# Wider input stages, value products beside five of them, and gathered rank products in a two-layer mixer on one Trainium2 core

## The chip, the core and the metric

The kernel runs on one core of a Trainium2 chip, in one launch. The time is device microseconds of that core, the median of several executions. PE or TensorE multiplies matrices, DVE (VectorE) and ACT (ScalarE) work on rows of 128 partitions, POOL is GpSimd, and SP's queue issues most of the DMA loads. A raw weight of fp32 is split into a high part and a remainder, both of the type fp32r, and one exact product costs three TensorE products: high times high, high times remainder, remainder times high.

## What is computed

The reference holds two layers. Only the start of the first one is touched here. With `x` and `ctx` of 256 tokens by 2048 channels each:

```python
sh, sc, gt = modulation(c_lat, w_ada[0], b_ada[0], 3)      # silu(c) @ w_ada + b_ada, 2048 channels each
sh_c, sc_c = modulation(c_c, w_ada[0], b_ada[0], 2)
u  = x   * (1.0 + sc)   + sh
uc = ctx * (1.0 + sc_c) + sh_c
k, v, rf, rb, q, gate_b, a_b, a_c, a_x, gate_a = split_cols(u @ w_in_e[0], E_SIZES)
k_c, v_c, rf_c, rb_c = split_cols(uc @ w_in_e[0][:, :2080], E_SIZES[:4])
```

`k` and `v` have 1024 columns, the gate ranks `rf` and `rb` 16 columns each. The keys, values and ranks are needed for `x` and for `ctx`; gated linear attention, a short convolution, an output projection with layer normalisation and the whole second layer follow.

## The kernel before, in words

The contraction over 2048 channels is done in 16 tiles of 128 (`KT`). The modulation of a channel tile has to be known before that tile's input can be multiplied with anything, so the first layer begins in stages, listed in `STAGES` (L58): 1, 1 and then seven times 2 channel tiles.

A stage has two halves. `stage_u` (L362) loads the columns of `x` and `ctx` that belong to its tiles (`load_xc`, L208), loads their shift and scale columns of `w_ada` and multiplies them with silu(c) (`mod_rows`, L264): units of 1 MB go through four raw buffers (`wraw`, L95), and the 16 contraction tiles are summed in four groups of output rows, the product of tile kt in group kt % 4. With n tiles in a stage a unit is 128 x n columns wide and holds 16 / n contraction tiles; a row of it in memory is 512 x n bytes. `to_cols` (L283) copies the four partial rows (ACT, L286) and turns them into columns (L289). Then each tile of the input is transposed (L386, L387), scaled and shifted (L389, L390) and split (L394 to L397). Whenever four tiles are done, the ranks of these four are multiplied (L398 to L409): four products of 32 columns, in the four row groups of one PSUM tile `pr`, and `r_acc` takes their sum.

`stage_k` (L411) multiplies the keys of a stage: two units of 512 columns, for each of them four token tiles (two of `x`, two of `ctx`) with 3 x n products, added into `knat` by DVE (L422). `v_fill` (L439) does the same with the first 512 columns of the values, for two contraction tiles at a time; `FILLS` (L41) puts it behind the stages that end at tiles 2, 4, 6 and 8, so 8 of the 16 contraction tiles are done there. Its split weights lie in buffers of their own (`wide`, L324); all others share four buffers for high parts and four for remainders, each of two contraction tiles by 512 columns (`whp`, `wlp`, L96, L97).

The loop at L563 sets the order: `w_ahead` loads and splits the two key units of the stage before, `stage_u` of this stage, `stage_k` of the stage before, then its fills. A load of values therefore stands behind the modulation weights of the next stage. SP issues the loads of weights in this order, and each waits for one of the four raw buffers. The order of the instructions on every engine is fixed ahead of the run by a scheduler that works with priorities (`prio`, L103) and planned times.

After the stages come the rest of the values (L768: for each half of the columns the units that no fill has done, here 2 and 4, 48 products each), the queries, the attention in the background, the convolution and the projection. Beside every unit of weights `tick` (L605) steps background work: `gate_gen` (L698) and later the attention by a budget, and the modulation of the second layer (`ada_accum`, L522, DVE) by `ada_credit`, 3 steps a unit in the values, fewer later; what is left is done at L1132, ahead of the first normalisation.

Of the kernel before, what the change touches and what calls it, by code (L numbers as in the profile page):

```python
# [9 lines left out]
F32 = mybir.dt.float32  # L10
# [3 lines left out]
ALU = mybir.AluOpType  # L14
# [3 lines left out]
P = 128  # L18
# [14 lines left out]
ADA_0 = {}  # L33
# [7 lines left out]
FILLS = {2: [(0, 0, 2)], 4: [(0, 2, 2)], 6: [(0, 4, 2)], 8: [(0, 6, 2)]}  # L41
FILL_PRIO = 0
# [15 lines left out]
STAGES = (1, 1, 2, 2, 2, 2, 2, 2, 2)  # L58
# [3 lines left out]
def kernel(  # L62
# [96 lines left out]
    # units in the order of their use; loads and splits run ahead of the products  # L159
# [71 lines left out]
    # columns 2, 3: silu of c and c_ctx; a window of 32 columns puts them on the rows 0, 1 or 2, 3 of a product  # L231
# [5 lines left out]
    # columns of colT: see the rows above  # L237
# [26 lines left out]
    def mod_rows(k0, n):  # L264
        """scale (rows 0, 1 of each group of 32) and shift (rows 2, 3) of n channel tiles, summed over every fourth contraction tile"""
# [70 lines left out]
    filled = [[kt + j for f in FILLS.values() for nb, kt, nk in f if nb == n for j in range(nk)] for n in range(2)]  # L336
    V_Q = [[q for q in range(4) if 4 * q not in filled[n]] for n in range(2)]
    for nb in range(2):
        block(W_E, 1024 + nb * 512, V_Q[nb])
# [22 lines left out]
    def stage_u(k0, n):  # L362
        w, n0 = n * P, k0 * P
        xc = xcs.pop(k0, None)
        if xc is None:
            xc = load_xc(k0, n)
        xs, cs = xc[:, 0:2, :], xc[:, 2:4, :]
# [11 lines left out]
        for j in range(n):  # L379
# [5 lines left out]
            for t in range(2):  # L385
                nc.tensor.transpose(out=px[:, t * P : (t + 1) * P], in_=xs[:, t, j * P : (j + 1) * P], identity=ident)  # L386
                nc.tensor.transpose(out=px[:, 256 + t * P : 256 + (t + 1) * P], in_=cs[:, t, j * P : (j + 1) * P], identity=ident)  # L387
# [10 lines left out]
            if i == 3:  # L398
                pr = mp([P, 512], "pr")
                for g in range(4):  # L400
                    kk = kt - 3 + g
                    nc.tensor.matmul(  # L402
                        out=pr[32 * g : 32 * g + 32, :], lhsT=wr[:, kk, :], rhs=quad_u[kk // 2][:, kk % 2, :],
                        start=True, stop=True,
                    )
                if q == 0:
                    nc.vector.tensor_copy(r_acc, pr)
                else:
                    nc.vector.tensor_tensor(out=r_acc, in0=pr, in1=r_acc, op=ALU.add)  # L409
# [13 lines left out]

    wps = []
# [11 lines left out]

    vnat = []

    def v_fill(nb, kt, nk):  # L439
        """a part of the values' contraction, for the gaps that the loads leave"""  # L440
        parts = w_next((W_E, kt, nk, 1024 + nb * 512), 0, 0)
        if not vnat:
            vnat.extend(slot([P, 1024], F32, "vnat") for _ in range(4))
        with prio(FILL_PRIO):
            for m in range(4):
                acc = acc_bank("vfill")
                for j in range(nk):
                    mm3(acc, utile(m, kt + j), parts[j], j == 0, j == nk - 1)
                dst = vnat[m][:, nb * 512 : (nb + 1) * 512]
                if kt == filled[nb][0]:  # L450
                    nc.scalar.copy(dst, acc)
                else:
                    nc.vector.tensor_tensor(out=dst, in0=acc, in1=dst, op=ALU.add)
# [21 lines left out]
    def ada_unit(layer, k0, n0):  # L475
        """four contraction tiles of the modulation's weights, two slots of two"""
# [26 lines left out]
    def ada_rows_gen(layer, dst, engs):  # L503
        """the gate of a layer, on every partition: products on DVE, the sum over the channels with ones"""
# [27 lines left out]
    def ada_cols_gen(layer, n0, dst, bias, one, engs, on_pe=()):  # L532
        """a section as channel columns: products on DVE, or on PE for the column blocks in on_pe"""
# [29 lines left out]
    for n in STAGES:  # L563
        if prev:
            w_ahead(2, SPLIT_0)
        stage_u(k0, n)
        if prev:
            stage_k(*prev)
            pump_ada(ADA_0.get(sum(prev), 0))
            for f in FILLS.get(sum(prev), ()):  # L570
                v_fill(*f)
        elif SPLIT_0:
            with tc.issue_after(arow_ins[0].ins):
                w_ahead(2, 2)
        prev = (k0, n)
        k0 += n
# [45 lines left out]
    def gemm_by_tile(groups, getu, done, budget=0.0, between=None, halves=False):  # L622
        """one token tile behind the other: the first one's sums are done while the second is at work"""
# [711 lines left out]
```

## Time and profile before

| | |
|---|---|
| three runs | 1018.31, 1018.49, 1013.9 us |
| median | 1018.31 us |
| span of the profiled execution | 1014.8 us |
| its own time beside the span | not listed apart; the span lies 3.5 us below the median and 0.9 us above the fastest run |
| TensorE busy | 973.4 us |
| DVE busy | 801.4 us |
| ACT busy | 463.3 us |
| read from memory | 252.41 MB |

All times in the rows below are microseconds from the start of the span. TensorE's records overlap, since one product starts while the one before it is still draining; its cost in a row of products is the distance of their starts. An fp32 product is recorded as two instructions, an fp32r product as one.

### The profile page before, as it was taken

How to read it: one execution, taken by the hardware profiler on the slowest of the kernel's cores; microseconds unless marked ns; L12 is line 12 of the kernel's file. 1: busy time of each engine (PE TensorE's matmuls, PEld its weight loads, DVE VectorE, ACT ScalarE, POOL GpSimd, SP SyncE). 2: the span in 40 equal slices, each digit the busy share in tenths (PEclk: the TensorE clock that was granted, in tenths of full speed). 3: DMA queues.
4: the chain of work that ended last, by engine and by line, in shares of the span. 5: the costliest groups of instructions: out<-in, count | busy, mean ns of one | idle time of the engine just before them, and what ended most of it. 6: DMA issues, size and time to landing. Idle time of an engine off the chain costs nothing.

```text
span 1014.8 us, 14425 instructions
## 1 busy us (share of the span) xinstructions
PE 973.4 (96%) x5718; PEld 768.6 (76%) x5718; DVE 801.4 (79%) x1161; ACT 463.3 (46%) x629; POOL 24.0 (2%) x55
## 2 busy tenths in 40 slices
PE   5899999999999999989999999999999999999995
PEld 4566666778878877877878788887888887778885
DVE  1555556989996999699999879987769968576676
ACT  2422214365684775336563444446554454454340
POOL 2000000000000000000000000000100001000000
PEclk9999999999999999999999999999999999999998
DMA  9987899667786676757767897984887888877532
GB/s 264 327 264 261 284 289 331 203 226 254 249 298 243 199 258 219 258 171 249 245 213 248 290 322 253 323 315 170 292 308 233 277 267 277 284 268 257 175 121 83
DMA packets 150373, 255.45 MB, mean 252 GB/s; under 512 B 5079, under 2 KB 46721, under 8 KB 150305
## 3 DMA queue, kind: packets, MB, share of 16 engines
q1 hardware_dynamic: 146592, 245.13, 72.3%
q0 software_dynamic: 2896, 8.72, 2.7%
q8 instruction: 45, 0.74, 0.3%
q10 hardware_dynamic: 816, 0.68, 0.3%
q14 instruction: 24, 0.19, 0.0%
HBM read 252.41 MB, written 2.10 MB: 251 GB/s over the span
## 4 chain that ended last, share of the span: by engine, by line
PE 43%; DVE 31%; DMA 19%; issue 4%; ACT 3%; SPq 0%; DVEq 0%; ACTq 0%
DMA raw<-in_w_ada_dram 16%; DVE wl L154 11%; DVE aacc L530 8%; PE oacc L191 5%; PE oacc L193 5%; PE oacc L192 5%; PE xacc L193 4%; PE xacc L192 4%; PE xacc L191 4%; PE ada L275 2%; PE kacc L191 2%; PE kacc L193 2%; PE kacc L192 2%; PE pr L402 1%; DMA raw<-in_w_in_e_dram 1%
## 5 line engine op out<-in xcount | busy, mean ns | idle before, releaser
L153 ACT CAST wh<-raw 128x1024 fp32r<-128x1024 f32 (+1 forms) x250 | 257.8, 1044 | 252.6 <-PE xacc L193 97.8
L154 DVE TENSOR_TENSOR wl<-raw,wh 128x1024 fp32r<-128x1024 f32 (+1 forms) x250 | 297.9, 1211 | 40.6 <-ACT wh L153 38.1
L530 DVE SCALAR_TENSOR_TENSOR aacc<-raw,sil,aacc 128x512 f32<-128x512 f32 x240 | 179.5, 748 | 42.6 <-DMA raw<-in_w_ada_dram 38.7
L191 PE MATMUL xacc<-wh,uxh 128*128 128x512 f32 x384 | 152.6, 397 | 0.0
L193 PE MATMUL xacc<-wh,uxl 128*128 128x512 f32 x384 | 151.8, 395 | 0.0
L192 PE MATMUL xacc<-wl,uxh 128*128 128x512 f32 x384 | 150.3, 391 | 0.1
L192 PE MATMUL xacc<-wl,u1h 128*128 128x512 f32 x240 | 94.4, 393 | 3.2 <-DVE wl L154 3.0
L191 PE MATMUL xacc<-wh,u1h 128*128 128x512 f32 x240 | 95.2, 397 | 0.8 <-ACT u1h L1156 0.8
L193 PE MATMUL xacc<-wh,u1l 128*128 128x512 f32 x240 | 93.7, 391 | 0.0
L192 PEld LDWEIGHTS xacc<-wl,uxh 128*128 128x128 f32 x384 | 72.1, 188 | 16.2 <-DVE wl L154 1.0
L193 PEld LDWEIGHTS xacc<-wh,uxl 128*128 128x128 f32 x384 | 72.2, 188 | 15.3 <-issue 0.2
L191 PEld LDWEIGHTS xacc<-wh,uxh 128*128 128x128 f32 x384 | 72.1, 188 | 15.5 <-ACT wh L153 0.5
L422 DVE TENSOR_TENSOR knat<-kacc,knat 128x512 f32<-128x512 f32 x64 | 42.8, 686 | 34.5 <-PE kacc L193 34.3
L192 PEld LDWEIGHTS xacc<-wl,u1h 128*128 128x128 f32 x240 | 45.1, 188 | 16.0 <-DVE wl L154 6.1
L191 PEld LDWEIGHTS xacc<-wh,u1h 128*128 128x128 f32 x240 | 45.1, 188 | 11.2 <-ACT u1h L1156 1.3
L193 PEld LDWEIGHTS xacc<-wh,u1l 128*128 128x128 f32 x240 | 45.1, 188 | 9.5 <-DVE u1l L1157 0.4
L286 ACT COPY arow<-ada 128x256 f32<-128x256 f32 (+1 forms) x9 | 3.1, 349 | 100.8 <-PE ada L275 100.8
L275 PE MATMUL ada<-raw,sil 128*32 128x256 f32 (+1 forms) x576 | 36.4, 382 | 10.8 <-DMA raw<-in_w_ada_dram 10.7
L191 PE MATMUL oacc<-wh,y1h 128*128 128x512 f32 (+1 forms) x120 | 45.5, 379 | 0.0
L193 PE MATMUL oacc<-wh,y1l 128*128 128x512 f32 (+1 forms) x120 | 45.0, 375 | 0.0
L192 PE MATMUL oacc<-wl,y1h 128*128 128x512 f32 (+1 forms) x120 | 45.0, 375 | 0.0
L275 PEld LDWEIGHTS ada<-raw,sil 128*32 128x32 f32 x576 | 17.3, 119 | 27.4 <-issue 12.6
(326 smaller groups left out, 1685.6 us busy)
## 6 DMA issues: line engine op xcount, KB each, us to landing
raw<-in_w_ada_dram SPq DMA_DIRECT2D x96, 1024.0 KB, 6.4
raw<-in_w_in_e_dram SPq DMA_DIRECT2D x54, 1024.0 KB, 5.7
raw<-in_w_in_o_dram SPq DMA_DIRECT2D x32, 1024.0 KB, 6.5
raw<-in_w_out_e_dram SPq DMA_DIRECT2D x16, 1024.0 KB, 7.0
raw<-in_w_out_o_dram SPq DMA_DIRECT2D x16, 1024.0 KB, 5.2
raw<-in_w_in_e_dram SPq DMA_DIRECT2D x18, 512.0 KB, 6.9
raw<-in_w_pool_dram SPq DMA_DIRECT2D x4, 1024.0 KB, 8.1
gt<-in_b_ada_dram POOLq DMA_DIRECT2D x8, 256.0 KB, 4.6
```

Of the source, the lines that this page charges most:

```text
L153: nc.scalar.copy(h, r[:, j : j + w, :])
L154: nc.vector.tensor_tensor(out=l, in0=r[:, j : j + w, :], in1=h.bitcast(F32), op=ALU.subtract)
L191: nc.tensor.matmul(out=acc, lhsT=uh, rhs=wh, start=start, stop=False)
L192: nc.tensor.matmul(out=acc, lhsT=uh, rhs=wl, start=False, stop=False)
L193: nc.tensor.matmul(out=acc, lhsT=ul, rhs=wh, start=False, stop=stop)
L275: nc.tensor.matmul(out=ps[32 * g : 32 * g + 32, :], lhsT=sil[:, kt, 2 - 2 * half : 34 - 2 * half], rhs=r[:, j, :], start=half == 0 and kt ...
L286: arow_ins.append(nc.scalar.copy(a[:, :nw], ps))
L402: nc.tensor.matmul(out=pr[32 * g : 32 * g + 32, :], lhsT=wr[:, kk, :], rhs=quad_u[kk // 2][:, kk % 2, :], start=True, stop=True,)
L422: nc.vector.tensor_tensor(out=dst, in0=acc, in1=dst, op=ALU.add)
L530: e.scalar_tensor_tensor(out=a, in0=r[j], scalar=sc, in1=a, op0=ALU.mult, op1=ALU.add)
```

## The change

The stages become 1, 1, 2, 4, 4, 4. In a four-wide stage a unit of modulation weights is 512 columns wide and holds four contraction tiles. The inputs of such a stage come as two loads of pairs. The values' first 512 columns are multiplied behind the keys of the first five stages, as wide as the stage (12 contraction tiles, of which the first is now behind the first stage), and their split weights use the shared buffers; the later part has 1 and 4 units left. The four rank products of a quarter are issued by `ranks`: the one of the last tile first, the other three behind it, at a raised priority. The values lie in tiles by column halves. All else in the diff is comments and texts taken out.

```diff
-FILLS = {2: [(0, 0, 2)], 4: [(0, 2, 2)], 6: [(0, 4, 2)], 8: [(0, 6, 2)]}
-FILL_PRIO = 0
+PR_PRIO = 200
+V_FILLS = 3
-STAGES = (1, 1, 2, 2, 2, 2, 2, 2, 2)
+STAGES = (1, 1, 2, 4, 4, 4)
...
             specs.append((W_E, k0, n, nb * 512))
+        if k0 + n <= 4 * V_FILLS:
+            specs.append((W_E, k0, n, 1024))
         k0 += n
-        for nb, kt, nk in FILLS.get(k0, ()):
-            specs.append((W_E, kt, nk, 1024 + nb * 512))
-            wide.add(len(specs) - 1)
...
-    for nb in range(2):
-        block(W_E, 1024 + nb * 512, V_Q[nb])
+    block(W_E, 1024, range(V_FILLS, 4))
+    block(W_E, 1536)
...
     def stage_u(k0, n):
-        w, n0 = n * P, k0 * P
-        xc = xcs.pop(k0, None)
-        if xc is None:
-            xc = load_xc(k0, n)
+        w = n * P
+        pairs = [(k, min(2, k0 + n - k)) for k in range(k0, k0 + n, 2)]
+        xts = [xcs.pop(k, None) for k, _ in pairs]
+        xts = [load_xc(*h) if t is None else t for t, h in zip(xts, pairs)]
...
             if i == 3:
-                pr = mp([P, 512], "pr")
-                for g in range(4):
-                    kk = kt - 3 + g
-                    nc.tensor.matmul(
-                        out=pr[32 * g : 32 * g + 32, :], lhsT=wr[:, kk, :], rhs=quad_u[kk // 2][:, kk % 2, :],
-                        start=True, stop=True,
-                    )
...
+                ranks(kt)
+
+    def ranks(kt):
+        pr = mp([P, 512], "pr")
+        def product(g):
+            kk = kt - 3 + g
+            return nc.tensor.matmul(
+                out=pr[32 * g : 32 * g + 32, :], lhsT=wr[:, kk, :], rhs=quad_u[kk // 2][:, kk % 2, :], start=True, stop=True)
+        with prio(-PR_PRIO):
+            first = product(3)
+            with tc.issue_after(first.ins):
+                for g in range(3):
+                    product(g)
...
+    def v_fill(k0, n):
+        parts = w_next((W_E, k0, n, 1024), 0, 0)
+        for m in range(4):
+            acc = acc_bank("vfill")
+            for j in range(n):
+                mm3(acc, utile(m, k0 + j), parts[j], j == 0, j == n - 1)
+            if k0 == 0:
+                nc.scalar.copy(vcols(m, 0), acc)
+            else:
+                nc.vector.tensor_tensor(out=vcols(m, 0), in0=acc, in1=vcols(m, 0), op=ALU.add)
...
             stage_k(*prev)
-            pump_ada(ADA_0.get(sum(prev), 0))
-            for f in FILLS.get(sum(prev), ()):
-                v_fill(*f)
+            if sum(prev) <= 4 * V_FILLS:
+                v_fill(*prev)
...
     for nb in range(2):
         accs = [acc_bank("vacc") for _ in range(4)]
-        gemm(W_E, 1024 + nb * 512, V_Q[nb], range(4), utile, accs, budget=B_V)
+        gemm(W_E, 1024 + nb * 512, range(V_FILLS if nb == 0 else 0, 4), range(4), utile, accs, budget=B_V)
```

## Rows read from the trace of the kernel before

**Rows 1.** The page: busy times, and TensorE and DMA in 40 slices.

```profile
PE 973.4 (96%) x5718; PEld 768.6 (76%) x5718; DVE 801.4 (79%) x1161; ACT 463.3 (46%) x629; POOL 24.0 (2%) x55
...
PE   5899999999999999989999999999999999999995
...
DMA  9987899667786676757767897984887888877532
```

**Rows 2.** Stages: length, busy PE, PEld, DVE, ACT, POOL (instructions), clock, DMA share, GB/s.

```profile
0.00:41.00 41.00, 27.18 (x254) 18.30 (x254) 11.89 (x29) 11.18 (x23) 7.04 (x17) 1.00 1.04 299
41.00:195.00 154.00, 151.61 (x940) 101.01 (x941) 96.62 (x173) 42.91 (x77) 0.41 (x2) 1.00 0.84 274
...
86.00:110.40 24.40, 23.85 (x147) 14.98 (x147) 13.74 (x23) 5.44 (x10) 0.00 (x0) 1.00 0.78 259
...
198.00:270.00 72.00, 71.70 (x326) 58.88 (x323) 65.80 (x96) 42.35 (x65) 0.51 (x5) 1.00 0.75 260
```

**Rows 3.** TensorE's timeline (start, duration): first and last of 24 value products.

```profile
95.98 0.39 PE L191 MATMUL vfill<-swh,uxh 128*128 128x512 f32 x1
...
101.20 0.39 PE L193 MATMUL vfill<-swh,ucl 128*128 128x512 f32 x1
```

**Rows 4.** TensorE's timeline: a unit of modulation weights between two key products.

```profile
80.06 0.39 PE L192 MATMUL kacc<-wl,uxh 128*128 128x512 f32 x1
80.38 1.07 PE L275 MATMUL ada<-raw,sil 128*32 128x256 f32 x16
81.39 0.50 PE L193 MATMUL kacc<-wh,uxl 128*128 128x512 f32 x1
```

**Rows 5.** TensorE's timeline: rank products of the second quarter.

```profile
87.04 1.05 PE L402 MATMUL pr<-u,wr_acc 128*32 128x512 f32 x4
...
88.36 0.40 PE L192 MATMUL kacc<-wl,uxh 128*128 128x512 f32 x1
88.69 1.04 PE L402 MATMUL pr<-u,wr_acc 128*32 128x512 f32 x2
89.67 0.50 PE L193 MATMUL kacc<-wh,uxl 128*128 128x512 f32 x1
90.00 0.40 PE L191 MATMUL kacc<-wh,uxh 128*128 128x512 f32 x1
90.33 1.05 PE L402 MATMUL pr<-u,wr_acc 128*32 128x512 f32 x2
```

**Rows 6.** TensorE's timeline: rank products of the first and the fourth quarter.

```profile
42.65 1.91 PE L402 MATMUL pr<-u,wr_acc 128*32 128x512 f32 x6
...
46.98 1.05 PE L402 MATMUL pr<-u,wr_acc 128*32 128x512 f32 x2
...
171.73 1.92 PE L402 MATMUL pr<-u,wr_acc 128*32 128x512 f32 x6
174.24 1.04 PE L402 MATMUL pr<-u,wr_acc 128*32 128x512 f32 x2
```

**Rows 7.** TensorE's timeline around 41 us; in brackets the idle time before and its releaser.

```profile
39.62 1.07 PE L275 MATMUL ada<-raw,sil 128*32 128x256 f32 x16 [1.88 <-DMA raw<-in_w_ada_dram]
41.18 0.61 PE L289 MATMUL adaT<-sel,arow 128*128 128x4 f32 x4 [0.49 <-ACT arow L286]
...
44.49 0.73 PE L191 MATMUL vfill<-swh,uxh 128*128 128x512 f32 x2
```

**Rows 8.** DMA packets of two stretches: 25 to 40 us, then 730 to 740 us.

```profile
DMA packets 4756, 5.28 MB, mean 352 GB/s; under 512 B 101, under 2 KB 4273, under 8 KB 4755
...
DMA packets 1834, 3.84 MB, mean 384 GB/s; under 512 B 89, under 2 KB 89, under 8 KB 1834
```

**Rows 9.** SP's timeline: loads of two key units and one values unit.

```profile
33.52 4.64 SPq L139 DMA_DIRECT2D raw<-in_w_in_e_dram  x3
```

**Rows 10.** The output projection, columns as in rows 2.

```profile
620.00:640.00 20.00, 20.00 (x90) 16.55 (x89) 18.69 (x25) 7.47 (x9) 0.00 (x0) 1.00 0.77 261
```

**Rows 11.** A wait of TensorE in the attention, and the stretch around it (columns as in rows 2).

```profile
434.46 0.41 PE L965 MATMUL yT<-ident,y 128*128 128x128 f32 x2 [3.63 <-DVE y L959]
...
430.00:440.00 10.00, 6.37 (x22) 4.47 (x21) 8.91 (x26) 2.64 (x4) 0.00 (x0) 0.83 0.34 106
```

More of the change, by code (lines that the diff above doesn't have):

```diff
@@ L384, in stage_u @@
             px = mp([P, 512], "px")
-            for t in range(2):
-                nc.tensor.transpose(out=px[:, t * P : (t + 1) * P], in_=xs[:, t, j * P : (j + 1) * P], identity=ident)
-                nc.tensor.transpose(out=px[:, 256 + t * P : 256 + (t + 1) * P], in_=cs[:, t, j * P : (j + 1) * P], identity=ident)
+            xc, c0 = xts[j // 2], (j % 2) * P
+            for t in range(4):
+                nc.tensor.transpose(out=px[:, t * P : (t + 1) * P], in_=xc[:, t, c0 : c0 + P], identity=ident)
             ux, uc = u[:, kt % 2, 0:256], u[:, kt % 2, 256:512]
@@ L398, in stage_u @@
             if i == 3:
-                pr = mp([P, 512], "pr")
-                for g in range(4):
-                    kk = kt - 3 + g
-                    nc.tensor.matmul(
-                        out=pr[32 * g : 32 * g + 32, :], lhsT=wr[:, kk, :], rhs=quad_u[kk // 2][:, kk % 2, :],
-                        start=True, stop=True,
-                    )
[L406 to L409, printed above, removed]
+                ranks(kt)
[10 more added lines that the diff above has]
+                    product(g)
+        if kt == 3:
+            nc.vector.tensor_copy(r_acc, pr)
+        else:
+            nc.vector.tensor_tensor(out=r_acc, in0=pr, in1=r_acc, op=ALU.add)
     def stage_k(k0, n):
@@ L422, in stage_k, with vcols @@
                     nc.vector.tensor_tensor(out=dst, in0=acc, in1=dst, op=ALU.add)
+    vns = {}
+    def vcols(m, nb, cs=slice(0, 512)):
+        if nb not in vns:
+            vns[nb] = [slot([P, 2, 512], F32, "vnat") for _ in range(2)]
+        return vns[nb][m // 2][:, m % 2, cs]
+    def v_fill(k0, n):
[6 more added lines that the diff above has]
+                nc.scalar.copy(vcols(m, 0), acc)
+            else:
+                nc.vector.tensor_tensor(out=vcols(m, 0), in0=acc, in1=vcols(m, 0), op=ALU.add)
     wps = []
@@ L435, in gate_weights @@
             wps.append(wp)
[L437 to L453, printed above, removed]
     ones = const([P, P], F32, "ones")
@@ L763 @@
         pass
-    if not vnat:
-        vnat.extend(slot([P, 1024], F32, "vnat") for _ in range(4))
     gg = gate_gen()
@@ L948, in gla_gen @@
             for h in range(2):
-                vs = slice((2 * hp + h) * 256, (2 * hp + h + 1) * 256)
-                terms = [(S[:, 2 * h + t, :], vnat[t]), (X[:, 2 * h + 1 - t, :], vnat[1 - t]),
-                         (C[:, 2 * h, isl], vnat[2]), (C[:, 2 * h + 1, isl], vnat[3])]
-                for n, (s_, v_) in enumerate(terms):
-                    nc.tensor.matmul(out=po[:, h, :], lhsT=s_, rhs=v_[:, vs], start=n == 0, stop=n == 3)
+                vs = slice(h * 256, (h + 1) * 256)
+                terms = [(S[:, 2 * h + t, :], t), (X[:, 2 * h + 1 - t, :], 1 - t), (C[:, 2 * h, isl], 2), (C[:, 2 * h + 1, isl], 3)]
+                for n, (s_, m) in enumerate(terms):
+                    nc.tensor.matmul(out=po[:, h, :], lhsT=s_, rhs=vcols(m, hp, vs), start=n == 0, stop=n == 3)
             ssq = small([P, 2], "ssq")
```

11 lines of the change are left out of this document (3 added, 8 removed).

## The prediction, made before the changed kernel was run

> **What bounds the kernel now.** I read the page first, its busy times and its forty slices. TensorE (PE) is busy 973.4 of 1014.8 us; only the first slice and the last lie far below nine tenths, and the DMA line has its nines in the first slices [rows 1]. So every later part can move the end only through TensorE's work, and the change touches the start. The table by stage says where: up to 41 us TensorE is busy 27.18 us while the DMA engines are full (share 1.04); from 41 to 195 us, in which the other keys are multiplied, it is busy 151.61 of 154 us and the DMA share is 0.84; in the values it is busy 71.70 of 72 us [rows 2]. The start waits for transfers, the rest for TensorE. Work that is only moved from the values to the keys' stages is therefore worth nothing, except where it falls into a hole.
>
> The price list of TensorE comes from its timeline. 24 products of one values part start from 95.98 to 101.20 us, 23 steps, so 0.227 us each [rows 3]; their durations of 0.39 us overlap. A megabyte of modulation weights is 16 records (two per fp32 product). From the product ahead to the one behind it pass 1.33 us, less the usual 0.23 is 1.10, and the next step is 0.1 late too: 1.2 us a unit [rows 4]. A rank product, squeezed in alone between two key products (two records), costs the same: from 88.36 to 90.00 us pass 1.64 us for two steps worth 0.46, so 1.18 us [rows 5].
>
> **The sum, part by part.** It is made against the profiled span, 1014.8 us. The median of the runs shown is 1018.3, 3.5 above it, and I add that at the end.
>
> Ranks as one group. The four products of a quarter go to four separate groups of output rows and can run together, which their prices show: six records take 1.91 us and two take 1.05 [rows 5, 6]. In the second quarter they come as 4, 2 and 2 records, three rounds [rows 5], and the third quarter repeats that; one round would do, so each gives back 2 x 1.18 = 2.4 us. In the fourth they come as 6 and 2: 1.92 less 1.05, and one lone round, together 2.05 us [rows 6]. That is **-6.8 us**. The first quarter has 6 and 2 as well, but its saving falls into the hole below and is counted there. The wait it adds: the group stands until the fourth tile's modulated input is made, and key products behind it in TensorE's order wait too. I take 0, because with four-wide stages the keys of the stage before are there to be put ahead of it; the other bound is a whole round, 1.05 us, four times.
>
> Fewer stages. Seven chains (modulation rows copied, turned to columns, input scaled and split) after 41 us become four, with as many transposes in all. With 432 products at 0.227 (98.1), 24 modulation units at 1.2 (28.8), the rank products (8 lone rounds at 1.18 and two pairs of rounds at 1.9, together 13.2) and seven chains at 1.5 (from 41.18 to 42.65, [rows 6, 7]) I get 150.6 of the 154 us. The rest, 3.4 us, is waiting around seven chains; three fewer give **-1.5 us**, between 0 and -3.4.
>
> Values beside the first stage. Twelve products of the first contraction tile can now stand in the hole ahead of 41 us, where TensorE waits 1.88 us for modulation weights and then for its chain [rows 7]: -2.7 us. Their 0.26 MB come ahead of the next modulation weights on SP's queue, 0.75 us at the 352 GB/s of that stretch [rows 8]; as they also hold one of four raw buffers, it may be a whole landing more, 3 us. I take 1.0, nearer the lower end as the queue was full: **-1.7 us**.
>
> The first four-wide stage. Here the change costs. Between the stage of tiles 2, 3 and that of tiles 4 to 7 the queue must bring 8.39 MB of modulation weights, 1.05 of inputs, 1.05 of keys and 0.26 of values: 10.75 MB, where two-wide stages had half of the weights. TensorE has a chain of 1.5, one round of ranks 1.1, 12 values products 2.7, 48 key products 10.9, eight modulation units 9.4 and 0.4 of small transposes: 26.0 us. The remaining 24 values products of tiles 2, 3 are no cover, since that load stands behind the weights in the program, as the part of tiles 0, 1 did: three w_in_e loads go out at 33.52 us and its products start at 44.49 [rows 7, 9]. The transfers take 30.5 us at 352 GB/s, the rate of packets of 1 KB, or 28.0 at the 384 of packets of 2 KB [rows 8]; the last weights' own products come after, so TensorE has 0.5 us less than that. Idle 4.0 or 1.5 us; as all but the inputs will be in 2 KB pieces I take 2.4, and 1.8 us for the chain that nothing covers (from 39.62 to 44.49 us pass 4.9, less 1.1 of weights' products, 1.5 of chain and 0.9 of a rank round, which leaves 1.4, and twice as many columns are copied). **+4.2 us**, between 2 and 8.
>
> A rule speaks against the wide weights. The Trainium skill (DMA: Bandwidth & Descriptors, Specifications) gives 512 B as the least transfer for line rate. By it 1 KB pieces are at the full rate already, and the 384 would have another cause. The trace has 352 against 384, in stretches that both ran full, so I go by the rows; the rule's result stands among the rivals.
>
> What costs nothing. A four-wide unit of weights is one round of 512 columns in place of two of 256: the same 1.2 us, 32 units in both kernels. Fewer additions into the keys' sums relieve VectorE (DVE), which was busy only 96.62 of those 154 us [rows 2]. SP issues 72 loads of the first layer's inputs and weights to the end of the values in place of 78; it was waiting for buffers, not issuing. The later values part is one unit of 11 us shorter, so three of its 18 background steps of the second layer's modulation move back, into the output projection: there DVE is busy 18.69 of 20 us while TensorE is full [rows 10]. I take 0; if that cover is gone, the last step is late at the first normalisation, one unit's 3 us of DVE, so +3.
>
> Sum: -6.8 - 1.5 - 1.7 + 4.2 = **-5.8 us**: a span of 1009.0, a median of 1012.5. Two kernels less than 0.5% (5.1 us) apart can't be told apart here.
>
> **The rivals.** *Nothing starves.* The scheduler finds other work for the hole, the early part doesn't delay the loads, and the rest waits less: -6.8 - 1.5 - 2.7 = -11.0, 1007.3 us. For it: the key stretch holds little idle time today [rows 2].
>
> *The ranks don't gather.* The first product is put ahead, but the others fall apart again by when their inputs are planned, or TensorE stands for the fourth tile as long as it saves. The -6.8 is gone: +1.0, 1019.3 us. For it: the order is planned before the run, and today's order planned them apart [rows 5]. Against: the diff chains three to the first.
>
> *Line rate from 512 B.* Weights run at 352 whatever their width: idle 4.0 in place of 2.4, a sum of -4.2, 1014.1 us. The section of the Trainium skill named above (DMA: Bandwidth & Descriptors) would have it so; the rows speak against it.
>
> *The first four-wide stage starves TensorE.* If the queue gets only the 274 GB/s of the whole key stretch [rows 2], 10.75 MB take 39.2 us: idle 12.7 and 1.8 for the chain. After a wait of 3.63 us the granted clock was 0.83 over ten microseconds, 1.7 us lost [rows 11], which would be added. The sum is then +6.2, 1024.5 us. It is even at about 310 GB/s and past half a per cent below about 282. For it: a four-wide unit of keys or values takes two of four split buffers of each kind, so raw tiles may wait longer and block loads. Against: the 274 was with TensorE as the bound (23.85 of 24.40 us in one such stage) and buffers waiting for it [rows 2]; when products were prompt, 352 was held for 15 us [rows 8].
>
> **How the numbers follow.** The forecast has 0.45; its own range is -8.5 to -3.5, 1009.8 to 1014.8, some two thirds of it past the 0.5%. Nothing starves 0.17, ranks 0.16, line rate 0.08, starving 0.14. Faster: 0.30 + 0.17 = 0.47; slower 0.14; same the rest, 0.39. The range runs from just past the second case to just past the third, 1006.0 to 1019.5, and leaves out the starving one and the tail of the fast one.
>
> **What would show it.** Right: rank products as four groups of 8 records, about 1.05 us each, and 150 us of key work shrinking to below 140 plus the moved values; a hole of 2 to 5 us ahead of the products of tiles 4 to 7, at 380 GB/s; values at 2.7 us in the hole ahead of 41. Wrong: lone pairs of rank records; a stretch of 10 us with half-idle TensorE between 44 and 75 us; a clock below 1.00 there; TensorE waiting for aacc or u1h at the first normalisation.

## The result and the profile after

The changed kernel took 1024.55 us (median of 20 executions, 1016.91 to 1027.24) beside 1018.25 us for the kernel before (20 executions, 1013.9 to 1022.61). The ratio is 1.0058, with a 95% interval of 1.0043 to 1.0072: slower by about 6 us. The forecast was 1012.5 us, the other way. The profiled execution of the changed kernel took 1024.47 us, of which its span is 1022.7.

The page of the changed kernel answers to [rows 1]; the PEclk line is the granted clock of TensorE in tenths.

```profile
PE 975.2 (95%) x5526; PEld 770.0 (75%) x5526; DVE 787.0 (77%) x1136; ACT 467.2 (46%) x629; POOL 24.1 (2%) x55
...
PE   5889999999899999999999899998999999999995
...
PEclk9899999999899999999999899999999999999998
DMA  9999887376658667767758778996887778877532
```

TensorE is as busy as before (975.2 for 973.4 us), but it has fewer records, and the clock line has eights that it should not have: in the second slice (25 to 51 us), in the eleventh (255 to 281 us) and in the twenty-third. Busy time that grows while the work shrinks is work at half the clock.

The table by stage, with the columns of [rows 2], of the kernel after:

```profile
0.00:41.00 41.00, 28.93 (x250) 20.36 (x250) 13.14 (x30) 13.44 (x27) 7.05 (x17) 1.00 0.98 276
41.00:75.00 34.00, 29.97 (x162) 16.70 (x162) 14.42 (x26) 5.32 (x10) 0.00 (x0) 0.90 0.96 336
75.00:117.00 42.00, 40.56 (x207) 25.06 (x204) 17.99 (x30) 10.59 (x19) 0.00 (x0) 0.96 0.96 338
117.00:198.00 81.00, 79.30 (x403) 57.59 (x402) 50.58 (x90) 25.44 (x41) 0.41 (x2) 1.00 0.67 227
198.00:270.00 72.00, 70.50 (x331) 57.75 (x329) 63.46 (x92) 37.61 (x57) 0.41 (x4) 1.00 0.70 236
...
275.00:300.00 25.00, 24.45 (x99) 20.07 (x100) 19.82 (x28) 19.09 (x30) 0.31 (x3) 0.87 0.49 165
```

The same two key stretches of the kernel before:

```profile
41.00:75.00 34.00, 33.72 (x201) 22.36 (x202) 19.93 (x36) 12.89 (x24) 0.00 (x0) 1.00 0.82 268
75.00:117.00 42.00, 41.45 (x268) 27.17 (x267) 22.28 (x41) 10.90 (x20) 0.00 (x0) 1.00 0.83 277
```

The stretch of the first four-wide stage shows both faults that the prediction named, a hole and a clock below 1.00: TensorE idles 4.0 of 34 us while the DMA share is 0.96, and the clock is 0.90 there and 0.96 in the next 42 us, where it was 1.00 before. The half clock costs 0.10 x 34 + 0.04 x 42 = 5.1 us of full-speed time. Of these the first 3.4 us, and a wait of 2.34 us, lie ahead of the wide stage's own hole, at the last modulation weights of tiles 2, 3 (42.5 to 49.4 us; the rows stand under the hardware below). The wide stage's own waits are 1.86 us for weights at 74.0 us and 0.70 us for the copied rows behind them.

To see where the whole 6 us arise I followed six records of TensorE's timelines, the start of each in the profiled executions:

| start of | before | after | after less before |
|---|---|---|---|
| the modulation columns (adaT) of tiles 2, 3 | 41.18 | 45.28 | +4.1 |
| the last product of the values | 268.98 | 268.37 | -0.6 |
| the 24th product of the queries | 275.80 | 283.78 | +8.0 |
| the 744th | 483.63 | 482.41 | -1.2 |
| the 360th product of the first output projection | 692.00 | 695.97 | +4.0 |
| the 24th product of the second layer (xacc number 1224) | 719.57 | 727.17 | +7.6 |

Up to the values' end nothing was won where 10 us were expected from ranks, fewer stages and early values, and 4.2 lost. Then 8.6 us are lost between the last value product and the queries. They are returned by 483 us, in part because the changed kernel has no such wait as [rows 11] at that place; it has one of 3.75 us at 573 us in its stead. Another 3.6 us are lost at the first normalisation. So there are three places to explain, and the wait for attention results that moves about.

**The second place** was new to me. TensorE's timeline of the kernel after, where the values end:

```profile
268.37 0.39 PE L192 MATMUL vacc<-wh,ucl 128*128 128x512 f32 x1
268.60 1.09 PE L724 MATMUL pz<-rp,wp 96*128 96x512 f32 x4
272.82 0.79 PE L724 MATMUL pz<-rp,wp 96*128 96x512 f32 x1 [3.13 <-ACT E L729]
274.13 0.80 PE L724 MATMUL pz<-rp,wp 96*128 96x512 f32 x1 [0.52 <-ACT E L729]
275.55 0.80 PE L190 MATMUL xacc<-wh,uxh 128*128 128x512 f32 x1 [0.62 <-ACT vnat L778]
276.14 0.63 PE L191 MATMUL xacc<-wl,uxh 128*128 128x512 f32 x1
276.57 0.63 PE L192 MATMUL xacc<-wh,uxl 128*128 128x512 f32 x1
```

ACT's timeline of the kernel after, at the same time:

```profile
273.94 1.08 ACT L730 ACTIVATE ga<-ga 128x1024 f32<-128x1024 f32 x1
274.89 0.61 ACT L778 COPY vnat<-vacc 128x512 f32<-128x512 f32 x1
```

And of the kernel before, where the last value product starts at 268.98:

```profile
262.92 1.08 ACT L725 ACTIVATE ga<-ga 128x1024 f32<-128x1024 f32 x1
263.87 0.60 ACT L776 COPY vnat<-vacc 128x512 f32<-128x512 f32 x1
```

The queries' first product needs a PSUM bank that holds finished values until ACT has copied it (vnat, L778). Before, the first copy runs 5 us ahead of the last value product, under TensorE's cover; after, it comes 6.5 us behind it, because the gates' activations stand ahead of it in ACT's fixed order. TensorE waits, and its products then start 0.43 us apart in place of 0.23, the half clock, to 281 us.

**The third place** shows in the column products of the second layer's modulation (adaS), which the first normalisation needs. This view lists one tile's records: count, least, median and greatest ns, first and last start. Before, then after:

```profile
L551 PE MATMUL adaS<-ones,aacc x64: 164/250/251, 222.4 to 670.2; 128*128 128x1 f32 x64
```

```profile
L557 PE MATMUL adaS<-ones,aacc x64: 164/250/271, 233.2 to 690.3; 128*128 128x1 f32 x64
```

The last one is 20 us later. It starts 5.7 us ahead of the 360th projection product, where it was 21.8 before, and the second layer's first products then wait in the kernel after as follows:

```profile
714.35 0.50 PE L190 MATMUL xacc<-wh,u1h 128*128 128x512 f32 x1 [1.66 <-ACT u1h L1157]
```

### The profile page after: what moved, and what is told of

Same layout as the page of the kernel before. It is cut to its first block, busy times and chain, and to the rows that moved or that the text cites. A ratio compares the mean times of both kernels' runs of the same rounds, so it can differ in the third digit from the quotient of the medians.

```text
span 1022.7 us, 13994 instructions
## 1 busy us (share of the span) xinstructions
PE 975.2 (95%) x5526; PEld 770.0 (75%) x5526; DVE 787.0 (77%) x1136; ACT 467.2 (46%) x629; POOL 24.1 (2%) x55
## 4 chain that ended last, share of the span: by engine, by line
PE 63%; DVE 17%; DMA 14%; ACT 3%; issue 2%; SPq 0%; DVEq 0%; ACTq 0%
DMA raw<-in_w_ada_dram 13%; PE xacc L190 8%; PE xacc L192 8%; PE xacc L191 8%; PE oacc L190 6%; PE oacc L192 6%; DVE wl L153 6%; PE oacc L191 6%; DVE aacc L536 5%; PE ada L274 2%; PE kacc L191 2%; PE kacc L192 2%; PE kacc L190 2%; PE vacc L190 1%; PE vacc L191 1%
## 5 line engine op out<-in xcount | busy, mean ns | idle before, releaser
L152 ACT CAST wh<-raw 128x1024 fp32r<-128x1024 f32 (+1 forms) x255 | 262.5, 1041 | 277.8 <-PE xacc L192 101.0
L153 DVE TENSOR_TENSOR wl<-raw,wh 128x1024 fp32r<-128x1024 f32 (+1 forms) x255 | 302.3, 1207 | 51.5 <-ACT wh L152 49.6
L426 DVE TENSOR_TENSOR knat<-kacc,knat 128x512 f32<-128x512 f32 x40 | 27.5, 690 | 39.5 <-PE kacc L192 39.4
L274 PE MATMUL ada<-raw,sil 128*32 128x512 f32 (+2 forms) x384 | 36.5, 501 | 12.1 <-DMA raw<-in_w_ada_dram 12.1
L285 ACT COPY arow<-ada 128x512 f32<-128x512 f32 (+2 forms) x6 | 2.7, 444 | 70.1 <-PE ada L274 70.1
L274 PEld LDWEIGHTS ada<-raw,sil 128*32 128x32 f32 x384 | 11.1, 124 | 26.4 <-issue 14.9
```

Source lines behind the costliest of these rows:

```text
L152: nc.scalar.copy(h, r[:, j : j + w, :])
L153: nc.vector.tensor_tensor(out=l, in0=r[:, j : j + w, :], in1=h.bitcast(F32), op=ALU.subtract)
L274: nc.tensor.matmul(out=ps[32 * g : 32 * g + 32, :], lhsT=sil[:, kt, 2 - 2 * half : 34 - 2 * half], rhs=r[:, j, :], start=half == 0 and kt ...
L285: arow_ins.append(nc.scalar.copy(a[:, :nw], ps))
```

## The experiments

"V" is the start of the last value product, "Q" that of the 24th query product, "N" the time from the 360th projection product to the 24th of the second layer, all from TensorE's timeline of the profiled execution, in us. Each ratio is to runs of the kernel before on the same chip, whose medians were 1016.92 to 1018.25 us; where it and the plain medians differ, both are given.

| kernel | median | ratio to before (95%) | V | Q less V | N | span |
|---|---|---|---|---|---|---|
| before | 1018.25 | 1 | 269.0 | 6.8 | 27.6 | 1014.8 |
| after | 1024.55 | 1.0058 (1.0043 to 1.0072) | 268.4 | 15.4 | 31.2 | 1022.7 |
| e1 ranks alone | 1006.70 | 0.9893 (0.9868 to 0.9917) | 258.1 | 6.8 | 27.6 | 1006.6 |
| e2 wide, loose ranks | 1028.60 | 1.0111 (1.0091 to 1.0132) | 277.0 | 14.4 | 30.9 | 1029.6 |
| e3 narrow | 1010.42 | 0.9930 (0.9904 to 0.9955) | 255.9 | 14.2 | 31.3 | 1006.8 |
| e4 values beside 8 tiles | 1022.80 | 1.0047 (1.0029 to 1.0065) | 270.1 | 14.2 | 27.7 | 1021.1 |
| e5 whole tiles, narrow | 1009.32 | 0.9932 (0.9905 to 0.9959) | 259.1 | 6.0 | 31.0 | 1007.3 |
| e6 whole tiles, wide | 1019.53 | 1.0028 (1.0012 to 1.0044) | 269.7 | 6.0 | 31.0 | 1016.0 |
| e7 late wide | 1018.63 | 1.0018 (0.9997 to 1.0039) | 262.0 | 14.1 | 30.9 | 1013.6 |
| e8 early load | 1018.82 | 1.0014 (0.9999 to 1.0028) | 262.8 | 15.4 | 30.9 | 1017.9 |
| e9 whole tiles, early load | 1013.28 | 0.9964 (0.9939 to 0.9989) | 263.2 | 6.0 | 31.0 | 1010.8 |
| e10 after, 18 steps | 1023.15 | 1.0056 (1.0034 to 1.0078) | 268.8 | 13.9 | 27.6 | 1021.5 |
| e11 = e9, 18 steps | 1010.40 | 0.9943 (0.9923 to 0.9964) | 260.9 | 6.8 | 27.6 | 1007.9 |
| e12 = e5, 18 steps | 1008.06 | 0.9910 (0.9884 to 0.9936) | 258.1 | 6.8 | 27.7 | 1004.3 |

### Each large part alone: e1, e2, e3

**e1**: the kernel before with the new `ranks`, nothing else.

```diff
+PR_PRIO = 200
...
-                pr = mp([P, 512], "pr")
-                for g in range(4):
...
+                ranks(kt)
```

> The kernel before with one part of the change: the four rank products of a quarter as one group. Both theories want the keys to end earlier by the lone rounds that go: the last key product starts at 194.2 us in the kernel before and should start at 186 to 188 us, with rank products as four groups of 8 records. Theory A (the change gains at the start and gives it back where the values end and the queries begin, because the values part is a unit shorter): this kernel keeps six units of values, so the gain lasts, 6 to 7 us faster than before, about 1011.5. Theory B (the holes of the first four-wide stages and the lower clock behind them cost what the ranks give): it has no such stages, also about 1011.5. Theory C (every edit of the start shifts the fixed order of the background work, and stalls of 5 to 9 us come and go by chance): the gain at the last key product is there, the end is anywhere from 1008 to 1022.

**e2**: the kernel after with the loop of the kernel before in place of `ranks`.

```diff
-                ranks(kt)
+                pr = mp([P, 512], "pr")
+                for g in range(4):
...
```

> The changed kernel with the rank products issued as before, each quarter in the order of its tiles. If the gathering gives 6.8 us, the last value product (268.4 us in the changed kernel) starts 5 to 7 us later, at 273 to 275, and theories A and B put the end at 1030 to 1032, 12 to 14 us slower than before. Theory C: the start is later by 5 to 7 us and the end anywhere from 1018 to 1034.

**e3**: the kernel after with two-wide stages; its early values are then units of one and two tiles.

```diff
-STAGES = (1, 1, 2, 4, 4, 4)
+STAGES = (1, 1, 2, 2, 2, 2, 2, 2, 2)
```

> The changed kernel with the stages of before (1, 1 and seven of 2); the values still stand beside the keys of 12 contraction tiles and the ranks are still gathered. Theory B: without the wide stages the hole at 72 to 76 us and its low clock are gone, 4 to 6 us earlier at the last value product than the changed kernel, and the end at 1018 or less. Theory A: the values part is still one unit shorter, so the stall of 8 us at the first queries stays, and the end is 1018 to 1022. Under B the first query products show no wait above 1 us that the changed kernel does not also have.

Measured: the gathered ranks alone win 1.07%, 10.9 us at V (269.0 to 258.1) and about as much at the end, where 6 to 7 us were expected; the last key product starts at 182.95 us, ahead of the expected 186 to 188. The groups of [rows 5, 6] became one, as in this row of the kernel after:

```profile
51.23 1.07 PE L402 MATMUL pr<-u,wr_acc 128*32 128x512 f32 x8
```

The grouped view from 41 to 200 us (count, busy us, mean ns, idle before) has the rank products of before at 12.2 us:

```profile
L402 PE MATMUL pr<-u,wr_acc 128*32 128x512 f32 x32 | 12.2, 605 | 0.0
```

and those of e1 at 4.3, with no idle time ahead of them (the total idle time up to V is the same within 0.3 us):

```profile
L408 PE MATMUL pr<-u,wr_acc 128*32 128x512 f32 x32 | 4.3, 604 | 0.0
```

With the wide stages in place the same gathering is worth less: e2 is 4.1 us slower than after by the medians, 5.4 by the ratios, and 8.6 at V (5 to 7 were expected, and an end of 1030 to 1032). The wide stages are what loses: with two-wide ones V comes 12.5 us earlier (268.4 to 255.9), where 4 to 6 were expected, and the kernel ends 1.3% sooner by the ratios. e3's table by stage has its clock at full speed in both stretches:

```profile
41.00:75.00 34.00, 31.66 (x220) 21.32 (x224) 22.50 (x41) 10.57 (x20) 0.00 (x0) 1.00 0.95 313
75.00:117.00 42.00, 42.00 (x279) 30.75 (x273) 26.72 (x45) 11.00 (x20) 0.00 (x0) 1.00 0.96 315
```

That e3 has no half clock there is partly luck. The narrow e5, described below, waits 2.70 us for the same weights of tiles 2, 3 and falls to half clock behind them, at 0.90 up to 75 us:

```profile
41.00:75.00 34.00, 31.50 (x193) 21.95 (x194) 20.16 (x38) 10.77 (x20) 0.00 (x0) 0.90 0.90 298
```

From 41 to 198 us TensorE idles 7.2 us after (4.03 + 1.44 + 1.70) and 3.4 in e3 (2.34 + 0.00 + 1.03). With the 5.1 us of half clock, which e3 has none of, that is 8.9 of the 12.5 us; the remaining 3.6 I did not place. Between e5 and e6, the other pair that differs in the stages alone, V is 10.7 us later.

e3 also tells that the second place has nothing to do with the wide stages: Q less V is 14.2 there too.

### Why the queries start late: e4, e5, e6

Two theories were left for the late copies: the shorter later values part (five units of weights in place of six), in which the same background work of the gates has less room, or the value tiles by column halves, which change when a tile comes free and so ACT's planned order.

**e4**: one early value unit fewer, so six units are left, as before.

```diff
-V_FILLS = 3
+V_FILLS = 2
```

> The changed kernel with values beside the keys of 8 contraction tiles in place of 12, so that the later part has six units again, 18 background steps of modulation and the budget of before for the gates. Theory A: the stall at the first queries (3.13 and 0.52 us of waiting on ACT and 6 us at half clock) is gone, the end 6 to 9 us earlier than the changed kernel, 1015 to 1018. Theory B: only the hole at 44 to 76 us matters, which this kernel has too; the end stays at 1022 to 1026. Theory C: anything, with no link between the stall and the number of units.

**e5** (on e3) and **e6** (on the kernel after): the value tiles as before the change, four of 1024 columns.

```diff
-        if nb not in vns:
-            vns[nb] = [slot([P, 2, 512], F32, "vnat") for _ in range(2)]
-        return vns[nb][m // 2][:, m % 2, cs]
+        if not vns:
+            vns[0] = [slot([P, 1024], F32, "vnat") for _ in range(4)]
+        return vns[0][m][:, nb * 512 + (cs.start or 0) : nb * 512 + cs.stop]
```

> The narrow kernel (stages of before, gathered ranks, values beside 12 tiles) with the values again in four tiles of all 1024 columns, as in the kernel before, in place of tiles by column halves. Theory D: all four kernels with value tiles by halves wait 4 to 5 us at the first queries and then run at half clock, 7 to 8 us between the last value product and the 24th query product, and the two with whole tiles do not, because the second half's tiles must wait for a free slot among 31 when the gates hold most, so that ACT's copies of the values are planned behind the gates' work and TensorE waits for ACT. With whole tiles the copies lie among the last value products again, the stall goes, and the kernel takes about 1003, 7 us less than the narrow one. Theory A (the shorter values part makes the stall): it still has one unit less, the stall stays, 1010. Theory C: no link, 1003 to 1015.

> The changed kernel with the values in four whole tiles. Theory D: the stall of 8 us at the first queries goes, and the holes of the wide stages stay: last value product at 268 as in the changed kernel, the 24th query product at 275 to 277 in place of 283.8, the end at 1016 to 1018. Theory A: unchanged, 1023 to 1026.

Measured: with six units the delay is still 14.2; with whole tiles it is 6.0 in both, though five units are left. The theory of the shorter part fell; it is the halves. In e6 ACT's first copy starts at 262.4 us, 7.4 ahead of the last value product. In e9, below, which has whole tiles and ends its values at 263.2, ACT's first copy is as far ahead of it:

```profile
254.90 1.09 ACT L730 ACTIVATE ga<-ga 128x1024 f32<-128x1024 f32 x1
255.85 0.61 ACT L778 COPY vnat<-vacc 128x512 f32<-128x512 f32 x1
```

What it is worth at the end depends on what follows, and the ends expected (about 1003 for e5, 1016 to 1018 for e6) were missed. Between the wide pair (e6 and after) the ratios are 0.30% apart, 3.1 us, and the medians 5.0. Between the narrow pair (e5 and e3) they are level, 0.9932 and 0.9930: e5's lead of 5.0 us at Q is gone by the 168th query product (306.4 against 305.2 us), after a wait of 3.04 us for ACT's qn at 296 us that e3 does not have. Why a late copy follows from halved tiles, step by step in the scheduler, I did not look into.

### Which part of the wide stages costs: e7, e8

**e7**: the width grows two stages later, when there is more work at hand to cover the jump.

```diff
-STAGES = (1, 1, 2, 4, 4, 4)
+STAGES = (1, 1, 2, 2, 2, 4, 4)
```

> The changed kernel with stages 1, 1, 2, 2, 2, 4, 4: the jump from two to four comes four tiles later. If a jump starves TensorE because one two-wide stage has too few products for 8.4 MB of modulation weights, the hole and the low clock move with it, to the products ahead of tiles 8 to 11 (about 115 us), and the last value product starts near 268 as in the changed kernel; if the wide stages are costly only while the start still fills, the hole is gone and it starts at 258 to 262. End: 1020 to 1025 under the first, 1012 to 1016 under the second.

**e8**: the order of the loads: in every stage the unit of values goes out ahead of the next stage's modulation weights. For the first wide stage these are the values of tiles 2, 3.

```diff
-            w_ahead(2, SPLIT_0)
+            w_ahead(3, SPLIT_0)
```

> The changed kernel with the values unit of a stage loaded together with its two key units, ahead of the next stage's modulation weights. If the hole at 70 to 76 us comes from the 24 values products of tiles 2, 3 standing behind the weights on the queue (5.5 us of work that could fill it), the hole shrinks below 1 us, the granted clock there is 1.00, and the last value product starts 4 to 8 us earlier than in the changed kernel, at 260 to 264; the end 1016 to 1020. If the loads bound this stretch, its modulation weights land later by the 0.5 MB moved ahead of them, and the sum is the same within 2 us.

Measured: both bring V forward by some 6 us (262.0 and 262.8) and the median by as much (5.9 and 5.7). In e7 no hole moved to 115 us: TensorE waits 0.71 us for the copied rows at 117.6 us and not for weights, and V lies at the edge of what the second theory gave; the end, 1018.63, is above its 1012 to 1016. e8 came out as its first theory had it. In the kernel after the queue had not been slow all along, it had stood still. The DMA rate in 40 slices of 43 to 74 us, and the packets:

```profile
GB/s 375 95 24 111 246 404 399 350 362 362 369 370 388 383 309 93 262 407 410 370 328 394 394 367 386 407 383 394 383 365 201 346 402 370 315 267 375 354 383 354
DMA packets 5734, 10.27 MB, mean 331 GB/s; under 512 B 216, under 2 KB 1240, under 8 KB 5732
```

The second to fourth slice, 43.8 to 46.1 us, are almost empty (24 to 111 GB/s), and a few later ones are thin. SP's timeline of the kernel after shows the stop:

```profile
33.27 7.35 SPq L138 DMA_DIRECT2D raw<-in_w_in_e_dram  x3
44.37 0.37 SPq L138 DMA_DIRECT2D raw<-in_w_ada_dram  x1
```

The third load of layer weights was issued by 40.6 us, and for 3.7 us no raw buffer came free for the first of the eight wide units of modulation weights. What SP waited for in between, from 40 to 44.3 us (us in total, times, longest), were the last weights of tiles 2, 3: their landing, then TensorE's products with them.

```profile
SPq L138 <- DMA raw<-in_w_ada_dram: 1.9, 1, 1.9
SPq L138 <- PE ada L274: 1.6, 1, 1.6
```

The stop is not the wide stage's doing. The narrow e3 stands just as long at the same place:

```profile
32.47 7.22 SPq L138 DMA_DIRECT2D raw<-in_w_in_e_dram  x3
43.35 0.37 SPq L138 DMA_DIRECT2D raw<-in_w_ada_dram  x1
```

In e8 and e9 the loads that follow are those of inputs, which need no raw buffer, and the slices stay full. The two waits of TensorE for weights at 42.5 and 74.0 us are gone in e8, and its clock is 1.00 from 41 to 75 us. Up to V e8 idles 2.1 us less than the kernel after and loses 3.4 us less to the half clock, which is its whole gain; the 3.4 are those behind the weights of tiles 2, 3. What stays is the wide stage's own chain: in e8 and e9 TensorE waits 0.70 us for the copied rows and 2.6 for the scaled input ahead of the rank products.

### Do the losses add: e9 to e12

**e9**: e6 and e8 together.

> The kernel after with both cures at once: the value tiles hold whole rows of 1024 columns again, and the first four-wide stage's values are loaded ahead of the next modulation weights, as in the run of that alone. If the two losses are separate (the half clock behind the transfers' holes up to 90 us, and the late value copies ahead of the queries), their gains add: against the changed kernel 5 to 6 us less at the last value product (about 263), 7 us and not 14 from there to the 24th query product (about 270), and a median of 1012 to 1015 us. If it is one loss that two cures reach (the same slack used twice), the last value product is at 263 but the median stays at 1018 to 1020, or the hole returns because whole value tiles hold more memory than halves and raw buffers come free later.

Measured 1013.28 us: 11.3 below the kernel after by the medians, where e6 alone gave 5.0 and e8 alone 5.7. The gains add (5.0 and 5.7 make 10.7): they are two separate losses.

**e10, e11, e12**: five units at 3.7 steps make 18 background steps of the second layer's modulation in the values, as six at 3 did before; on the kernel after, on e9 and on e5.

```diff
-ADA_V = 3
+ADA_V = 3.7
```

> The kernel after with 3.7 in place of 3 background steps a unit in the values, so that the five units that are left do 18 steps, as the six did before. So far the three kernels with six units took 27.6 us from the 360th projection product of the first layer to the 24th product of the second layer, and the eight with five units took 30.9 to 31.3. Theory (the three steps that moved back make the normalisation's columns late): the distance is 27.6 again, the last column product of the second layer's modulation starts near 675 and not 690, and the median falls by 3 us, to about 1021. Rival (it is the order around the normalisation, which merely falls out this way where the values part is shorter): the distance stays at 31 and the median at 1024. Cost that either may have: VectorE has 18 steps beside a values part of 55 us in place of 66, and the last value product may come 0 to 3 us later.

> Wide stages, whole value tiles, early load of the values and 18 steps in the values: the three losses that the rows show, all mended, with the change otherwise as it was. If the three are separate, 3 us below the run with two of them mended: 1010, ratio about 0.993. If the steps fill VectorE in the values, the gain at the normalisation is lost there and it stays at 1013.

> Two-wide stages with gathered ranks, values beside six of the stages, whole value tiles and 18 steps in the values. If the steps are worth 3 us in every kernel with five units left, 1006 (ratio about 0.990), level with the ranks alone on the kernel before (0.9893). That would say that neither the wide weights nor the longer early values bring anything here beyond the gathered ranks.

Measured: N is 27.6 to 27.7 in all three, and the last column product of e10 starts at 670.9 us, as before:

```profile
L557 PE MATMUL adaS<-ones,aacc x64: 164/250/250, 233.5 to 670.9; 128*128 128x1 f32 x64
```

So the theory of the late columns holds without exception: the kernels with 18 steps in the values (before, e1, e4, e10, e11, e12) take 27.6 or 27.7 us there, those with fewer 30.9 to 31.3. At the end less than these 3.4 us is left: 1.4, 2.9 and 1.3 us by the medians, within the uncertainty of each. The second layer takes some of it back: from its 24th product to the end of the span e10, e11 and e12 take 301.2, 298.8 and 303.1 us, the same kernels with fewer steps 295.5, 297.0 and 295.8. e12 reaches that product 10.6 us ahead of e1 (701.2 to 711.8 us) and ends only 2.4 ahead by the spans; TensorE waits there for DVE, at the split weights (wl) up to 2.3 us at a time and once 2.6 us for the gate, and why I did not look into. e12 at 0.9910 cannot be told from e1 at 0.9893, and V is 258.1 in both: beyond the gathered ranks, early values beside the stages (seven of them in e12, not the six that the expectation names) bring nothing here. With everything mended, wide stages (e11, 0.9943) are not ahead of narrow ones either.

**The best version** is e1, the kernel before with the ranks as one group: 1006.70 us, 1.1% below the kernel before and 1.7% below the kernel after by the medians; e12 is level with it within the uncertainty.

## Why the prediction was wrong

By the ratios the change comes apart into steps that follow one another: ranks alone 0.9893 (-10.9 us of 1018); early values in shared buffers, five units left (e5) 0.9932 (+4.0, the intervals overlap); wide stages (e6) 1.0028 (+9.8); halved value tiles (after) 1.0058 (+3.1). Together these are the measured 0.58%.

**Ranks as one group, -6.8: right in kind, too small.** Four groups of 8 records came out as forecast, and no wait showed ahead of them. It gave 10.9. By the distances from start to start up to V, the rank products themselves take 7.5 us less (11.5 to 4.0), the first quarter among them, which had been left to the hole; the key products 2.4 less (96.9 to 94.5), as fewer of them stand beside a rank round; the rest is spread.

**Fewer stages and the first four-wide stage, -1.5 and +4.2, together +2.7: this is the step that failed.** They cost 9.8 us at the end (e5 to e6), and 10.7 (e5 to e6) or 12.5 (e3 to after) at V. The size of the hole was not far off: TensorE idles 3.8 us more than with narrow stages. But the sum went by a queue that runs without a stop at 384 GB/s; it ran at 331 over 31 us, with a stop at the start that the narrow kernel has too and that the wide stage, with 8.4 MB to come behind it, cannot spare. And the half clock behind a hole was in the rival alone: 5.1 us, more than the hole; 3.4 of them stand at the weights of tiles 2, 3, where a narrow kernel may lose them too, as e5 does. A hole of TensorE has to be priced with the clock that may follow it.

The wide stages' own cost was put too low as well. e11 has no stop and full clock up to V, and still starts its last value product 2.8 us behind the narrow e12 (260.9 to 258.1), which lost 1.7 us to the half clock on the way: some 4.5 us at V by this estimate. One sign in the sum is doubtful, too: products that come after the last weights cover no transfer, so the 0.5 us for them would lengthen the idle time (5.0 or 2.5 us) and not shorten it.

**The clock, over all executions.** The granted clock is on record for each. Its median is 0.984 over the 20 executions of the kernel after, and 0.992 to 0.995 for the four sets of the kernel before. The span times what is missing to 1, an estimate of the time lost at half speed, is 16.3 us after and 5.1 to 8.1 before; the rest of the span is 1007.0 us after and 1008.5 to 1009.3 before (medians). Each is an upper estimate, as half clock during a wait costs nothing. By them the whole loss is clock: at full clock the change would be level or 2 us ahead, still short of the 5.8 forecast. The same estimate splits the step from e5 to e6 into 2.6 us of clock and 7.2 of other time, so the wide stages are slower without the clock too.

**Values beside the first stage, -1.7: worth nothing.** They went into the hole (the busy time up to 41 us grew by 1.75 us against [rows 2], of the 2.7 forecast), but the delay of the loads was not 1.0: the modulation columns of tiles 2, 3 started at 44.1 in e3 and 45.3 after, against 41.1 in e1. That is 3 to 4 us, at and past the bound of a whole landing.

**The value tiles by column halves had no term at all.** The change's description names them, and the sum does not. They cost 8 to 9 us at the queries' start, and 3 at the end of the wide kernel by the ratios, nothing at that of the narrow one.

**Background steps, at 0 with a bound of +3: the bound was the better number.** The place (the first normalisation) and the sign to look for (TensorE waiting for u1h) were right: 3.6 us there, of which the runs leave 1.3 to 2.9 at the end, none of them clear of the uncertainty.

**The rival of the starving stage gave 1024.5 us, which is what came out, but not by its sum.** It had 12.7 us of idle time at 274 GB/s and 1.7 of clock. Idle time and clock were 3.8 and 5.1 us above e3, and two losses that it did not have make up the rest. Its reason, four-wide units of keys or values that hold the split buffers so that raw tiles wait, is not what stopped the queue at 40.6 us: SP waited there for the last weights of tiles 2, 3, and e3 has the stop without any four-wide unit. Its break-even of 310 GB/s leaves out the 1.7 us of clock that its 282 holds; with them it would be about 326. Of the signs named, the clock below 1.00 and the wait for u1h appeared; a stretch of 10 us with half-idle TensorE did not.

With early loads and whole tiles the change takes 1013.28 us, next to the forecast of 1012.5. That is agreement by cancellation: the ranks gave 4 us more than forecast, and what is left of the other losses took it back.

## What to carry to other kernels

Gather products of few columns that share the array into one group before anything else, and measure that alone: it was the whole gain here, and the parts beside it hid it. When units of a load get wider, look for stops of the queue just ahead of the jump and for the buffers that it waits for there, not only at the bytes, and price each hole of the bounding engine with the half clock that may follow. In a kernel whose order is planned ahead, an edit without arithmetic, such as the shape of a result tile or one unit less to hang background steps on, deserves a term of its own. Compare the granted clock of all executions before explaining a difference of half a per cent by work.

## What the runs showed of the hardware

**The length of a wait does not decide the clock.** In the kernel after, a wait of 2.34 us was followed by half speed: the value products behind it start 0.43 us apart.

```profile
39.13 1.07 PE L274 MATMUL ada<-raw,sil 128*32 128x256 f32 x16
42.54 1.79 PE L274 MATMUL ada<-raw,sil 128*32 128x256 f32 x16 [2.34 <-DMA raw<-in_w_ada_dram]
...
45.28 0.85 PE L288 MATMUL adaT<-sel,arow 128*128 128x4 f32 x4
...
48.16 0.63 PE L192 MATMUL vfill<-wh,uxl 128*128 128x512 f32 x1
48.59 0.63 PE L191 MATMUL vfill<-wl,uxh 128*128 128x512 f32 x1
```

In e3 a longer one, 2.96 us at the same place behind the same products, was not; there they start 0.23 us apart. (In e5 one of 2.70 us at that place was.)

```profile
38.19 1.07 PE L274 MATMUL ada<-raw,sil 128*32 128x256 f32 x16
42.22 1.07 PE L274 MATMUL ada<-raw,sil 128*32 128x256 f32 x16 [2.96 <-DMA raw<-in_w_ada_dram]
...
45.62 0.39 PE L192 MATMUL vfill<-wh,uxl 128*128 128x512 f32 x1
45.85 0.40 PE L191 MATMUL vfill<-wl,uxh 128*128 128x512 f32 x1
```

The wide stage's chain gives the same picture. e9 runs the rank products at half speed behind its wait,

```profile
80.22 1.94 PE L402 MATMUL pr<-u,wr_acc 128*32 128x512 f32 x8 [2.62 <-DVE u L385]
```

and e11, whose wait there is the same, at full speed:

```profile
79.74 1.06 PE L402 MATMUL pr<-u,wr_acc 128*32 128x512 f32 x8 [2.63 <-DVE u L385]
```

The granted clock from 75 to 117 us is 0.92 in e9 and 1.00 in e11. The two levels are 1.2 and 2.4 GHz, and which of them follows such a wait was not settled by any run here. The Trainium skill (TensorE: Matmul & The Clock Gate, What's actually happening) says that the monitor behind the clock does not start anew with a kernel, so that the moment of a change differs from run to run. That would fit the pair e9 and e11; no run here shows it by itself.

**Pieces of 2 KB ran faster than pieces of 1 KB while the queue was full**: 378 GB/s over 20 us of e9's wide loads (44 to 64 us; in e8 367),

```profile
DMA packets 4364, 7.57 MB, mean 378 GB/s; under 512 B 167, under 2 KB 1191, under 8 KB 4362
```

against 348 in the kernel before (50 to 61 us; its last 2 us are thinner, and [rows 8] has 352 in a full stretch).

```profile
DMA packets 3136, 3.83 MB, mean 348 GB/s; under 512 B 95, under 2 KB 2456, under 8 KB 3135
```

These stretches side with [rows 8]; the rule of the Trainium skill that the prediction weighed against them (DMA: Bandwidth & Descriptors, Specifications) would have both at one rate, and the measurement decides. The wider weights load some 4 to 7% faster here, and it did not make up for the waits and the half clock.
